# A diffusion layer on one core: the latent convolution in 32x32 tiles of the array, the layer norm by channels, and the scan's decay rows on ScalarE's queue

## The chip, the core and the metric

The kernel runs on one core of a Trainium2 chip. A core has five engines with instruction queues of their own: TensorE (PE; its weight loads are shown as PEld), VectorE (DVE), ScalarE (ACT), GpSimd (POOL) and SyncE (SP), which only issues transfers here. Transfers run on 16 DMA engines. The metric is the device time of one execution in microseconds (us), the median of several runs.

## The reference

One layer of a hybrid backbone, for 256 context tokens and 2048 latent tokens (a grid of 32 rows by 64 columns), model width 1024. Both go through the same weights:

```python
h = rms_norm(x, g_pre) * (1 + scale) + shift
u = h @ w_in
z, xbc, dt_raw, ga, gb, gsil = jnp.split(u, [...], axis=-1)
y_ssd, h_fin = ssd_branch(z, xbc, dt_raw, ...)          # scan in chunks of 128 tokens, both directions
# conformer_branch:
h = ga * jax.nn.sigmoid(gb)
h = depthwise_conv(h, conv_w, conv_b)                   # 31 taps along the grid's rows
h = layer_norm(h, ln_g, ln_b)                           # over the 1024 channels of a token
y_conf = jax.nn.silu(h) * jax.nn.silu(gsil)
out = jnp.concatenate([y_ssd, y_conf], axis=-1) @ w_out
return x + gate * rms_norm(out, g_post), h_fin
```

For latent tokens the convolution runs down the 32 rows of the grid, for each channel and each of 64 columns by itself. With 31 taps every one of the 32 rows reaches nearly every other, so one channel is a 32x32 matrix applied to a 32x64 block.

## The kernel before

Tokens are 18 tiles of 128 (two of context, 16 latent). The wide projections are made in three matmuls of 128x512 for each block of the contraction (high and low part of the operand: `mm_cm`, lines 378 to 380), the output projection likewise (`out_part`, line 1078: 96 matmuls a tile). The stages, by the trace:

- to about 340 us: modulation, normalised input, the scan's input channels for half 0 of the tokens (ten tiles);
- 340 to 720: `ga`, `gb` and the gates of half 0 (`gab_unit`, `silu_unit`); between their matmuls the scan of tiles 0 to 8 (`pass_a`) and half of the context convolution are interleaved;
- 720 to 945: the scan's channels for half 1;
- 945 to 1340: `ga`, `gb` and gates of half 1, interleaved with the scan of tiles 9 to 17, the latent convolution (`lat_conv`, eight channel blocks of 128) and the rest of the context convolution (`ctx_conv`);
- 1340 to 1430: the last gates, and `w_out` loaded and split;
- 1430 to the end: the final loop over 18 tiles: finish the scan's output (`ssd_pre`, `ssd_norm`, `ssd_scale`), normalise the convolution's (`conf_pre`, `conf_act`), project, add.

The names that matter below: `kd` is the kernel matrix data of a channel block as loaded, `kbuf` its expansion to block-diagonal 128x128 matrices of four channels (16 ScalarE copies of 32 partitions a block, line 622; the buffers are zeroed once by POOL), `cx` the block's input, `cp` the PSUM bank that a group of eight matmuls fills (line 634: the input is stationary, 128x64, the matrix moves), `cvv` the result with bias (line 639). The result has tokens on partitions and is stored as rows of tokens, `CVL`; for context `CVC`, after two transposes (line 595). In the final loop `conf_pre` loads a tile's tokens `cn`, takes mean and variance with VectorE's statistics instructions (1042, 1044), scales (1047), and `conf_act` transposes to channels with eight matmuls (1058) and applies SiLU with gain and bias from PSUM (1061).

In the scan, `load_lb` (line 664) broadcasts four decay rows to a tile `lb` of 128x512, 144 loads in all, eight a tile; POOL masks one direction (676), ScalarE takes exponentials (684, 673), VectorE multiplies (688), PE uses them as weights (720). `lb` has four buffers a direction.

All transfers are issued by SP, in order. The order of work on each engine is set by a scheduler that simulates the engines when the program is built; the interleaving of the source (`interleave`, `merge`) is what it starts from.

## Time and profile before

| | |
|---|---|
| median of 3 runs | 1882.09 us (1880.9 to 1887.08) |
| the profiled execution | 1882.2 us, span 1880.5 us |
| granted TensorE clock, mean | 0.986 |
| DMA, mean over the span | 200 GB/s, 375.29 MB |

"Busy" counts an engine's working instructions; waiting and the issue of transfers aren't counted. In a group row stand the source line, the engine, the operation, output and inputs, shapes, the count, then busy us and mean ns of one, then the idle time of the engine just before such instructions and what ended most of it. An fp32 matmul leaves two records, so the count of matmul records is twice that of instructions for those; the 128x512 matmuls of the projections and the transposes leave one. `SPq` is SP's own queue.

### The profile page before, as it was taken

Reading aid. Unit: us, or ns where it says so; the run is one execution under the profiler, and the core shown is the slowest. Engines: PE = TensorE matmul, PEld = TensorE weight load, DVE = VectorE, ACT = ScalarE, POOL = GpSimd, SP = SyncE. Lnnn points to the kernel's source line nnn. Section 1 sums busy time; section 2 is a strip of 40 time slices with the busy share of each in tenths; the row PEclk is TensorE's granted clock in tenths of the full one; section 3 lists DMA queues with packets and bytes.
Section 4 is the critical chain, followed back from the end, with each engine's and each line's share of the span. In section 5 each row is a group of like instructions: output and inputs, shape, how many; then the busy total and the mean of one; then the engine's idle time right before and its main releaser. Section 6 shows DMA issues by size and latency. Waiting matters only on the chain.

```text
span 1880.5 us, 26833 instructions
## 1 busy us (share of the span) xinstructions
PE 1825.6 (97%) x9739; PEld 1504.6 (80%) x9739; DVE 1188.2 (63%) x1699; ACT 839.5 (45%) x1786; POOL 269.0 (14%) x351
## 2 busy tenths in 40 slices
PE   7899999999999999999999899999999999999998
PEld 4788887787887888888877677777887888888887
DVE  2477887776545553577585768655427676766662
ACT  3646424443455441644355666675414232232321
POOL 0002001111111100100001011110013333333220
PEclk9899999999999999999999999999999999999999
DMA  8556575564677754545587897978887655555532
GB/s 302 212 200 198 211 239 179 176 222 155 211 269 225 225 200 169 165 154 188 179 195 215 210 242 194 278 185 234 239 268 239 191 174 173 165 172 173 175 102 78
DMA packets 290400, 375.29 MB, mean 200 GB/s; under 512 B 85206, under 2 KB 187478, under 8 KB 290268
## 3 DMA queue, kind: packets, MB, share of 16 engines
q1 hardware_dynamic: 290268, 373.58, 64.2%
q8 instruction: 77, 1.26, 0.3%
q14 instruction: 55, 0.45, 0.1%
HBM read 243.92 MB, written 129.59 MB: 199 GB/s over the span
## 4 chain that ended last, share of the span: by engine, by line
PE 62%; DMA 5%; ACT 3%; issue 3%; DVE 2%; SPq 2%; POOL 0%; POOLq 0%; DVEq 0%; ACTq 0%
PE op L1078 20%; PE sp L378 6%; PE sp L379 6%; PE sp L380 6%; DMA lb<-lt 3%; PE xp L379 2%; PE xp L378 2%; PE xp L380 2%; PE py L720 2%; PE ga L378 2%; PE ga L380 1%; PE po L727 1%; PE ga L379 1%; PE qo L985 1%; PE gb L378 1%
## 5 line engine op out<-in xcount | busy, mean ns | idle before, releaser
L684 ACT ACTIVATE lb<-lb,WB 128x128 f32<-128x128 f32 x576 | 184.1, 391 | 150.9 <-POOL lb L676 149.0
L378 PE MATMUL sp<-hh,wh 128*128 128x512 f32 (+1 forms) x640 | 239.7, 375 | 2.6 <-DVE sth L550 2.6
L379 PE MATMUL sp<-hl,wh 128*128 128x512 f32 (+1 forms) x640 | 237.0, 370 | 0.0
L380 PE MATMUL sp<-hh,wl 128*128 128x512 f32 (+1 forms) x640 | 236.7, 370 | 0.2 <-DMA wl<-wld 0.2
L676 POOL TENSOR_SCALAR_AFFINE_SELECT lb<-lb 128x512 f32<-128x512 f32 x144 | 108.7, 760 | 749.7 <-ACT el L673 416.1
L378 PE MATMUL xp<-hh,wh 128*128 128x512 f32 (+1 forms) x480 | 179.1, 375 | 6.1 <-ACT wh L353 4.0
L379 PE MATMUL xp<-hl,wh 128*128 128x512 f32 (+1 forms) x480 | 179.1, 373 | 0.2 <-DVE hl L299 0.2
L380 PE MATMUL xp<-hh,wl 128*128 128x512 f32 (+1 forms) x480 | 179.2, 374 | 0.0
L475 DVE SCALAR_TENSOR_TENSOR cva<-raw,cwh,cva 128x1280 f32<-128x1280 f32 (+1 forms) x96 | 142.7, 1495 | 15.5 <-ACT cva L469 13.6
L378 PEld LDWEIGHTS sp<-hh,wh 128*128 128x128 f32 x640 | 121.0, 189 | 24.3 <-DVE sth L550 3.1
L380 PEld LDWEIGHTS sp<-hh,wl 128*128 128x128 f32 x640 | 121.0, 189 | 21.6 <-DMA wl<-wld 0.7
L379 PEld LDWEIGHTS sp<-hl,wh 128*128 128x128 f32 x640 | 121.2, 189 | 20.1 <-issue 0.5
L378 PE MATMUL gb<-hh,wh 128*128 128x512 f32 (+1 forms) x320 | 121.9, 381 | 3.4 <-DVE gth L539 3.4
L378 PE MATMUL ga<-hh,wh 128*128 128x512 f32 (+1 forms) x320 | 120.4, 376 | 2.6 <-ACT gth L536 2.6
L379 PE MATMUL gb<-hl,wh 128*128 128x512 f32 (+1 forms) x320 | 119.3, 373 | 0.0
L380 PE MATMUL gb<-hh,wl 128*128 128x512 f32 (+1 forms) x320 | 119.1, 372 | 0.0
L380 PE MATMUL ga<-hh,wl 128*128 128x512 f32 (+1 forms) x320 | 118.1, 369 | 0.0
L379 PE MATMUL ga<-hl,wh 128*128 128x512 f32 (+1 forms) x320 | 117.9, 369 | 0.0
L590 DVE SCALAR_TENSOR_TENSOR cg<-cg,cv 128x256 f32<-128x256 f32 x240 | 113.3, 497 | 2.5
L550 DVE SCALAR_TENSOR_TENSOR sth<-sth,sp 128x512 f32<-128x512 f32 (+1 forms) x80 | 50.4, 630 | 98.4 <-ACT sth L549 98.4
L378 PEld LDWEIGHTS xp<-hh,wh 128*128 128x128 f32 x480 | 92.0, 192 | 23.0 <-ACT wh L353 4.8
L688 DVE TENSOR_TENSOR lb<-lb,lb 128x512 f32<-128x512 f32 x72 | 51.6, 717 | 85.6 <-ACT lb L684 55.8
(219 smaller groups left out, 3860.8 us busy)
## 6 DMA issues: line engine op xcount, KB each, us to landing
lb<-lt SPq DMA_DIRECT2D x144, 256.0 KB, 4.2
wr<-in_w_in SPq DMA_DIRECT2D x88, 256.0 KB, 4.9
whd<-wh SPq DMA_DIRECT2D x44, 512.0 KB, 3.4
wld<-wl SPq DMA_DIRECT2D x44, 512.0 KB, 4.7
wh<-whd SPq DMA_DIRECT2D x44, 512.0 KB, 5.2
wl<-wld SPq DMA_DIRECT2D x44, 512.0 KB, 5.6
xT<-xb SPq DMA_DIRECT2D x18, 512.0 KB, 5.4
yp<-yg SPq DMA_DIRECT2D x36, 256.0 KB, 4.5
```

The lines of the kernel that those rows point to most:

```text
L378: T.matmul(ps[:, :BN], wh[:, k, :], hh[:, k, :], start=(k == 0), stop=False)
L379: T.matmul(ps[:, :BN], wh[:, k, :], hl[:, k, :], start=False, stop=False)
L380: T.matmul(ps[:, :BN], wl[:, k, :], hh[:, k, :], start=False, stop=(k == KT - 1))
L475: V.scalar_tensor_tensor(a[:, :n], raw[:, t:t + n], cwh[:, ct * 5 + t:ct * 5 + t + 1], a[:, :n], MUL, ADD)
L550: V.scalar_tensor_tensor(th, th, 1.0, ps[:, :BN], ADD, MUL)
L590: V.scalar_tensor_tensor(acc, g[:, t:t + 256], cv[:, w0 + t:w0 + t + 1], acc, MUL, ADD)
L676: G.affine_select(E[g, hq, d], E[g, hq, d], pattern=[[0, 4], [sg, P]], compare_op=ALU.is_ge, fill=NEG, base=0, channel_multiplier=-sg)
L684: S.activation(lb[:, h, :], lb[:, h, :], AF.Exp, bias=WB[:, i, c + h:c + h + 1])
L688: V.tensor_tensor(a, a, E[g, hq, 1], ADD)
L720: T.matmul(py[g][j * HD:(j + 1) * HD, q * P:(q + 1) * P], xt[g][:, h * HD:(h + 1) * HD], E[g, hq, 0][:, t, :], start=True, stop=True)
L727: T.matmul(po[g][:, q * P:(q + 1) * P], Sf[g][:, q * P:(q + 1) * P], bc[:, 2 + g, :], start=True, stop=True)
L1078: T.matmul(pso[n], lhs[:, k % 8, :], w[:, n * 512:(n + 1) * 512], start=(k == 0 and m == 0), stop=(k == 15 and m == 2))
```

## The change

Three things are changed.

**The latent convolution.** Each matrix of 32x32 is now used as it is: stationary, on one 32x32 tile of the array, with the channel's input (32x64) moving. Partitions of `kd` and `cx` hold four groups `a` of channels with 32 rows of the grid each; the output's partitions are four groups `u`. A channel block is two half-groups of 64 matmuls: eight positions `q`, four `u` (columns of the array), two `a` (rows of the array, each into a PSUM bank of its own). One ScalarE copy a block turns the kernel around (`kt`); `cx` comes in 16 transfers, `kd` in 4, both for the next block ahead if its `GL` is complete; the bias is loaded once. The result has channels on partitions and goes to one tensor `CV` of channels by tokens, in 8 transfers a block. `ctx_conv` writes its rows there without transposes.

**The layer norm.** A tile is loaded with channels on partitions (`conf_load`), eight blocks of 128 tokens. `conf_mean` folds the eight blocks in three VectorE additions (`sum8`), adds over partitions and spreads the sum with one matmul against ones, and subtracts. `conf_var` squares (ScalarE), folds, and makes the variance a column of one value per token with a matmul of one column; POOL takes the power −1/2. `conf_scale` turns the column into a row on all partitions with a matmul against the identity, and multiplies. SiLU then reads SBUF. `ssd_pre`'s sum of squares uses `sum8` too, where it had one reduction (line 991).

**The decay rows.** `load_lb` issues from ScalarE's queue.

The body of `lat_conv` that goes stands in the listing above and is not repeated. Two spacers in memory and the places at which `out_part` is divided are changed with it.

```diff
     ZS = [dram(f"zs{h}", [D, HT[h] * P]) for h in range(2)]
     GL = [dram(f"gl{j}", [P, NT * P]) for j in range(KT)]
     GS = [dram(f"gs{h}", [D, HT[h] * P]) for h in range(2)]
-    CVC = dram("cvc", [NCTX * P, D])
-    CVL = dram("cvl", [LAT, D])
+    CV = dram("cv", [D, NT * P])
...
                 yield
-        ps = bank("ss", f"cps{j}")
-        for t in range(2):
-            T.transpose(ps[:, t * P:(t + 1) * P], acc[:, t * P:(t + 1) * P], ident)
         o = g[:, 768:1024]
-        S.mul(o, ps[:, :256], 0.5)
-        DMA.dma_start(CVC[:, j * P:(j + 1) * P].rearrange("(t p) c -> p t c", p=P),
-                      o.rearrange("p (t c) -> p t c", c=P))
-        yield
+        S.mul(o, acc, 0.5)
+        DMA.dma_start(CV[j * P:(j + 1) * P, 0:256], o)
...
+    def lat_load(j, lp):
+        kd = lp.tile([P, 32, 32], F32, tag="kd", name=f"kd{j}", bufs=2)
+        x = lp.tile([P, 32, 64], F32, tag="cx", name=f"cx{j}", bufs=2)
+        lat_in[j] = kd, x
+        for a in range(4):
+            rs = slice(a * 32, (a + 1) * 32)
+            src = bass.AP(tensor=wconv.tensor, offset=(j * 4 + a) * 64 * 32, ap=[[32, 32], [1, 1024]])
+            DMA.dma_start(kd[rs].rearrange("p r g -> p (r g)"), src)
+            for u in range(4):
+                c0 = u * 32 + a * 8
+                DMA.dma_start(x[rs, u * 8:(u + 1) * 8, :],
+                              GL[j][c0:c0 + 8, 256:].rearrange("c (r w) -> r c w", w=64))
+    def lat_conv(j, lp, cbb, more):
+        if j not in lat_in:
+            lat_load(j, lp)
+        kd, x = lat_in.pop(j)
+        yield
+        kt = lp.tile([P, 32, 32], F32, tag="kt", name=f"kt{j}", bufs=1)
+        S.copy(kt[:, :, ::-1].rearrange("p g r -> p r g"), kd)
+        if more(j + 1):
+            lat_load(j + 1, lp)
+        yield
+        vt = lp.tile([P, 32, 64], F32, tag="cvv", name=f"cvv{j}", bufs=1)
         for h in range(2):
+            ps = {a: bank("ss", f"cp{j}_{a}") for a in (2 * h, 2 * h + 1)}
+            for q in range(8):
+                for u in range(4):
+                    for a in ps:
+                        rs = slice(a * 32, (a + 1) * 32)
+                        T.matmul(ps[a][u * 32:(u + 1) * 32, q * 64:(q + 1) * 64], kt[rs, u * 8 + q, :], x[rs, u * 8 + q, :],
+                                 start=True, stop=True)
             yield
+            for a in ps:
+                V.scalar_tensor_tensor(vt[:, a * 8:(a + 1) * 8, :], ps[a].rearrange("p (c w) -> p c w", w=64), 0.5,
+                                       cbb[:, j, a * 8:(a + 1) * 8].unsqueeze(2).to_broadcast([P, 8, 64]), MUL, ADD)
+            for u in range(4):
+                c0 = j * P + u * 32 + h * 16
+                DMA.dma_start(CV[c0:c0 + 16, 256:].rearrange("c (r w) -> r c w", w=64),
+                              vt[u * 32:(u + 1) * 32, h * 16:(h + 1) * 16, :])
...
@@ -661,7 +663,7 @@
             for d in range(2):
                 lb = pa.tile([P, 4, P], F32, tag=f"lb{d}", name=f"lb{i}{g}{hq}{d}", bufs=4)
                 r0 = il * 32 + d * NH + g * 8 + hq * 4
-                DMA.dma_start(lb.rearrange("p h l -> p (h l)"),
+                S.dma_start(lb.rearrange("p h l -> p (h l)"),
                               LT[half][r0:r0 + 4, :].rearrange("h l -> (h l)").partition_broadcast(P))
...
-    kbuf = [lp.tile([P, 8, P], F32, name=f"kbuf{u}") for u in range(2)]
-    for u in range(2):
-        G.memset(kbuf[u], 0.0)
+    cbb = lp.tile([P, 8, 32], F32, name="cbb")
+    for u in range(4):
+        DMA.dma_start(cbb[u * 32:(u + 1) * 32],
+                      conf_b.rearrange("(j u n) -> u j n", u=4, n=32)[u].partition_broadcast(32))
     blocks = post(1, 5)
     cg = lambda name: lp.tile([P, D], F32, tag="cg", name=name, bufs=2)
-    extra = chain(f for j in range(4) for f in (lat_conv(2 * j, lp, kbuf), ctx_conv(j + 4, cg), lat_conv(2 * j + 1, lp, kbuf)))
+    lat = lambda j: lat_conv(j, lp, cbb, gl_done.__contains__)
+    extra = chain(f for j in range(4) for f in (lat(2 * j), ctx_conv(j + 4, cg), lat(2 * j + 1)))
...
+    def sum8(t, v):
+        V.tensor_tensor(t, v[:, 0:4, :], v[:, 4:8, :], ADD)
+        V.tensor_tensor(t[:, 0:2, :], t[:, 0:2, :], t[:, 2:4, :], ADD)
+        V.tensor_tensor(t[:, 0, :], t[:, 0, :], t[:, 1, :], ADD)
+        return t[:, 0, :]
...
-        zr = p1.tile([P, P], F32, tag="zr", name=f"zr{i}", bufs=2)
-        V.tensor_reduce(zr, z.rearrange("p q l -> p l q"), mybir.AxisListType.X, ADD)
+        zr = sum8(z[:, 0:4, :], z)
...
-    def conf_pre(i):
-        n = p2.tile([P, D], F32, tag="cn", name=f"cn{i}", bufs=1)
-        DMA.dma_start(n, CVC[i * P:(i + 1) * P, :] if i < 2 else CVL[(i - 2) * P:(i - 1) * P, :])
-        bs = p2.tile([P, 12], F32, tag="bs", name=f"bs{i}", bufs=2)
-        for h in range(2):
-            V.bn_stats(bs[:, 6 * h:6 * h + 6], n[:, h * 512:(h + 1) * 512])
-        mv = p2.tile([P, 2], F32, tag="mv", name=f"mv{i}", bufs=2)
-        V.bn_aggr(mv, bs)
-        V.tensor_scalar(mv[:, 1:2], mv[:, 1:2], EPS, None, ADD)
-        r = rstd_of(p2, mv[:, 1:2], f"cr{i}")
-        V.tensor_scalar(n, n, mv[:, 0:1], r, SUB, MUL)
+    rows8 = lambda t: t.unsqueeze(1).to_broadcast([P, 8, P])
+    def conf_load(i):
+        n = p2.tile([P, 8, P], F32, tag="cn", name=f"cn{i}", bufs=1)
+        DMA.dma_start(n, CV[:, i * P:(i + 1) * P].rearrange("(c p) t -> p c t", p=P))
         return n
 
-    def conf_act(i, n):
+    def conf_mean(i, n):
+        v = p2.tile([P, 8, P], F32, tag="v", name=f"v{i}", bufs=1)
+        t = sum8(v[:, 0:4, :], n)
+        mean = bank("ss", f"cm{i}")[:, 0:P]
+        T.matmul(mean, ones, t, start=True, stop=True)
+        V.scalar_tensor_tensor(n, rows8(mean), -1.0 / D, n, MUL, ADD)
+        return n, v
+    def conf_var(i, nv):
+        n, v = nv
+        S.activation(v, n, AF.Square)
+        t = sum8(v[:, 0:4, :], v)
+        pq = bank("ss", f"cq{i}")
+        T.matmul(pq[:, 0:1], t, ones[:, 0:1], start=True, stop=True)
+        ms = p2.tile([P, 1], F32, tag="cms", name=f"cms{i}", bufs=2)
+        V.tensor_scalar(ms, pq[:, 0:1], 1.0 / D, EPS, MUL, ADD)
+        return n, v, rstd_of(p2, ms, f"cr{i}"), pq
+    def conf_scale(i, nvr):
+        n, v, r, pq = nvr
+        T.matmul(pq[:, P:2 * P], r.to_broadcast([P, P]), ident, start=True, stop=True)
+        V.tensor_tensor(n, n, rows8(pq[:, P:2 * P]), MUL)
+        return n, v
+    def conf_act(i, nv):
+        n, v = nv
         gs = p2.tile([P, 8, P], F32, tag="gs", name=f"gsl{i}", bufs=1)
         DMA.dma_start(gs, chan_slice(GS, i))
-        v = p2.tile([P, 8, P], F32, tag="v", name=f"v{i}", bufs=1)
-        for g in range(2):
-            ps = bank("ss", f"ct{i}{g}")
-            for c in range(4):
-                k = 4 * g + c
-                T.transpose(ps[:, c * P:(c + 1) * P], n[:, k * P:(k + 1) * P], ident)
-            for c in range(4):
-                k = 4 * g + c
-                S.activation(v[:, k, :], ps[:, c * P:(c + 1) * P], AF.Silu, bias=cv[:, C_LNB + k:C_LNB + k + 1],
-                             scale=cv[:, C_LNG + k:C_LNG + k + 1])
+        for k in range(8):
+            S.activation(v[:, k, :], n[:, k, :], AF.Silu, bias=cv[:, C_LNB + k:C_LNB + k + 1],
+                         scale=cv[:, C_LNG + k:C_LNG + k + 1])
         V.scalar_tensor_tensor(v, v, 0.5, gs, MUL, MUL)
...
+                gap(p2, 64)
                 yh = ssd_scale(i, yr)
-                nrm = conf_pre(i)
+                nrm = conf_mean(i, conf_load(i))
...
-    v = conf_act(i, nrm)
+    v = conf_act(i, conf_scale(i, conf_var(i, nrm)))
...
-            n = conf_pre(nxt)
-        out_part(pso[i], yh, 3, 6)
+            n = conf_load(nxt)
+        out_part(pso[i], yh, 3, 5)
         if not last:
             yhn = ssd_scale(nxt, yr)
-        out_part(pso[i], yh, 6, 8)
+        out_part(pso[i], yh, 5, 7)
+        if not last:
+            n = conf_mean(nxt, n)
+        out_part(pso[i], yh, 7, 8)
         out_part(pso[i], pt, 8, 10)
         if last:
             out_part(pso[i], pt, 10, 16, (0,))
             out_part(pso[i], pt, 10, 16, (1,))
         else:
-            v = conf_act(nxt, n)
-            out_part(pso[i], pt, 10, 16)
+            n = conf_var(nxt, n)
+            out_part(pso[i], pt, 10, 12)
+            v = conf_act(nxt, conf_scale(nxt, n))
+            out_part(pso[i], pt, 12, 16)
...
-    wconv = wpad.reshape(8, 32, 4, 64).transpose(0, 2, 3, 1)
+    wconv = wpad.reshape(8, 4, 4, 8, 64).transpose(0, 2, 4, 1, 3)
```

In the second scan stage, on TensorE, the convolution stands between matmuls of the projection (`ga`, `hh`, `hl`, `wh`, `wl`; the changed kernel's lines 377 to 379 are 378 to 380 of before). Before:

```order
L380 MATMUL ga_1_4_8687<-hh_7343,wl_1_8345 128x512
L634 MATMUL cp_0_8691<-kbuf_8337,cx_8634 64x128 x8
L378 MATMUL ga_1_4_8687<-hh_7343,wh_1_8346 128x512
L379 MATMUL ga_1_4_8687<-hl_7344,wh_1_8346 128x512
L380 MATMUL ga_1_4_8687<-hh_7343,wl_1_8345 128x512
```

After:

```order
L379 MATMUL ga_1_4_8681<-hh_7330,wl_1_8333 128x512
L637 MATMUL cp_0_8686<-cx_8615,kt_8642 32x64
L637 MATMUL cp_1_8687<-cx_8615,kt_8642 32x64
L637 MATMUL cp_0_8686<-cx_8615,kt_8642 32x64
L637 MATMUL cp_1_8687<-cx_8615,kt_8642 32x64
```

The two banks alternate to 64 matmuls in one run, and then the projection goes on; there are 16 such runs where there were 32 of eight.

On ScalarE, in the first scan stage (`xwh` is a cast of the scan's input, `el` the exponential kept for later, `gth` a gate's eviction). Before:

```order
L710 CAST xwh_4602<-xw_4601 128x512
L673 ACTIVATE el_4680<-lb_4761 64x256 x2
L684 ACTIVATE lb_4761<-lb_4761,WB 128x128 x4
L710 CAST xwh_4669<-xw_4668 128x512
L749 COPY sb_4755<-pst_4660 128x512
```

After:

```order
L712 CAST xwh_4102<-xw_4101 128x512
L675 ACTIVATE el_4180<-lb_4244 64x256 x2
L686 ACTIVATE lb_4244<-lb_4244,WB 128x128 x4
L538 ACTIVATE gth_6_1_4135<-gb_6_1_4077 128x512
L666 DMA lb_4756<-lt_115 128x512
L686 ACTIVATE lb_4756<-lb_4756,WB 128x128 x4
L666 DMA lb_4296<-lt_115 128x512
L712 CAST xwh_4169<-xw_4168 128x512
```

The loads of `lb`, which stood on SP, stand between ScalarE's exponentials, casts and evictions.

On TensorE in the final loop (`op` the output's two banks, `yh`, `yl`, `ph`, `pl` the operands' parts, `pm` the scan norm's sums, `ct` the transposed tile, `cq` the variance and its spread). Before, the eight transposes:

```order
L1078 MATMUL op_0_14882<-woh_13066,pl_14879 128x512
L1078 MATMUL op_1_14883<-woh_13066,pl_14879 128x512
L1058 MATMUL ct_15002<-ident,cn_14940 128x128 x4
L1058 MATMUL ct_15011<-ident,cn_14940 128x128 x4
L1078 MATMUL op_0_14882<-woh_13072,ph_14878 128x512
```

After, around the spread of the scale:

```order
L1100 MATMUL op_1_15636<-wol_13435,yh_15517 128x512
L1074 MATMUL cq_15562<-ident,cr_15566 128x128
L1100 MATMUL op_0_15635<-woh_13436,yl_15518 128x512
L1100 MATMUL op_1_15636<-woh_13436,yl_15518 128x512
L1100 MATMUL op_0_15635<-woh_13475,yh_15517 128x512
```

The transposes are gone; the matmul of the variance stands ahead of the scan's `pm` and `qo`, that of the scale eight matmuls behind them, and before a tile's `ph` part the first matmuls of the next tile (`op_0` alone) are placed.

More of the change, by code (lines that the diff above doesn't have):

```diff
@@ L526, in xbc_phase @@
             pass
+    gl_done = set()
     def gab_unit(half, j, hb):
@@ L530, in gab_unit @@
         wa = next_w()
+        gl_done.discard(j)
         for b in ORDER[half]:
@@ L540, in gab_unit @@
             DMA.dma_start(GL[j][:, o:o + BN], th)
+        if half:
+            gl_done.add(j)
     def silu_unit(half, c0, dst, j, hb, order=None):
@@ new lines, in backbone_kernel @@
+    lat_in = {}
+    def lat_load(j, lp):
[10 more added lines that the diff above has]
+                              GL[j][c0:c0 + 8, 256:].rearrange("c (r w) -> r c w", w=64))
@@ new lines, in lat_conv @@
+    def lat_conv(j, lp, cbb, more):
[9 more added lines that the diff above has]
+        vt = lp.tile([P, 32, 64], F32, tag="cvv", name=f"cvv{j}", bufs=1)
+        for h in range(2):
+            ps = {a: bank("ss", f"cp{j}_{a}") for a in (2 * h, 2 * h + 1)}
[5 more added lines that the diff above has]
+                                 start=True, stop=True)
+            yield
+            for a in ps:
[5 more added lines that the diff above has]
+                              vt[u * 32:(u + 1) * 32, h * 16:(h + 1) * 16, :])
+            yield
@@ L1035, in load_gg @@
         gg[a] = t
-    def conf_pre(i):
-        n = p2.tile([P, D], F32, tag="cn", name=f"cn{i}", bufs=1)
-        DMA.dma_start(n, CVC[i * P:(i + 1) * P, :] if i < 2 else CVL[(i - 2) * P:(i - 1) * P, :])
-        bs = p2.tile([P, 12], F32, tag="bs", name=f"bs{i}", bufs=2)
-        for h in range(2):
-            V.bn_stats(bs[:, 6 * h:6 * h + 6], n[:, h * 512:(h + 1) * 512])
-        mv = p2.tile([P, 2], F32, tag="mv", name=f"mv{i}", bufs=2)
-        V.bn_aggr(mv, bs)
-        V.tensor_scalar(mv[:, 1:2], mv[:, 1:2], EPS, None, ADD)
-        r = rstd_of(p2, mv[:, 1:2], f"cr{i}")
-        V.tensor_scalar(n, n, mv[:, 0:1], r, SUB, MUL)
-        return n
@@ L1126, in backbone_kernel @@
                 p2 = ph_1.enter_context(tc.tile_pool(name="p2", bufs=1))
-                gap(p2, 192)
+                gap(p2, 64)
                 yh = ssd_scale(i, yr)
-                nrm = conf_pre(i)
+                nrm = conf_mean(i, conf_load(i))
     for u in last:
         run(u)
-    v = conf_act(i, nrm)
+    v = conf_act(i, conf_scale(i, conf_var(i, nrm)))
     ph_b[2].close()
```

36 lines of the change are left out of this document (removed).

## The prediction

> **What bounds the kernel now.** I read the busy shares first, then the chain of waits, then the windows by stage. The columns of the first row are busy us, share of the span, instructions.
>
> ```profile
> PE 1825.6 (97%) x9739; PEld 1504.6 (80%) x9739; DVE 1188.2 (63%) x1699; ACT 839.5 (45%) x1786; POOL 269.0 (14%) x351
> PE 62%; DMA 5%; ACT 3%; issue 3%; DVE 2%; SPq 2%; POOL 0%; POOLq 0%; DVEq 0%; ACTq 0%
> ```
>
> TensorE is busy 97% of the 1880.5 us span; no other engine passes 63%. The chain agrees: most of it is PE, and all else on it is small. So a change can win by taking work off PE, or by closing PE's pauses, and loses by opening new ones. The windows say where pauses are (first and last us, length, busy us of each engine with instructions, granted clock, DMA share, GB/s):
>
> ```profile
> 440.00:560.00 120.00, 117.72 (x676) 98.50 (x675) 62.54 (x110) 59.00 (x147) 15.82 (x21) 1.00 0.68 223
> 560.00:700.00 140.00, 137.37 (x776) 115.16 (x776) 76.11 (x126) 70.03 (x176) 13.43 (x19) 0.99 0.66 215
> 945.00:1060.00 115.00, 109.87 (x634) 85.79 (x633) 91.60 (x172) 65.03 (x147) 11.78 (x18) 0.97 0.78 196
> 1060.00:1200.00 140.00, 131.59 (x813) 103.97 (x812) 92.89 (x150) 91.01 (x213) 17.47 (x27) 0.98 0.86 226
> 1200.00:1340.00 140.00, 136.09 (x818) 106.09 (x817) 81.26 (x118) 88.06 (x191) 13.29 (x19) 0.99 0.79 226
> 1500.00:1600.00 100.00, 100.00 (x498) 84.35 (x497) 68.99 (x81) 28.96 (x60) 33.87 (x28) 1.00 0.58 178
> PE cp L634 <- ACT kbuf L622: 10.0, 6, 2.7
> PE cp L634 <- DMA cx<-gl: 1.9, 1, 1.9
> ```
>
> In the second scan stage (945 to 1340) PE idles 395 − 377.55 = 17.5 us, and the two wait rows (us, times, longest) give 11.9 of it to the latent convolution, which waits for its expanded kernel or its input. In the first scan stage (440 to 700) PE idles 4.9 us. In the final loop (1500 to 1600) it has no pause at all: there only fewer or shorter matmuls help.
>
> **The convolution on PE.** A group before is 8 matmuls, each with two records, in two column halves of the array:
>
> ```profile
> 957.30 0.39 PE L379 MATMUL ga<-hl,wh 128*128 128x512 f32 x1
> 957.53 0.39 PE L380 MATMUL ga<-hh,wl 128*128 128x512 f32 x1
> 957.85 1.09 PE L634 MATMUL cp<-kbuf,cx 128*64 128x128 f32 x16
> 958.87 0.50 PE L378 MATMUL ga<-hh,wh 128*128 128x512 f32 x1
> 959.21 0.40 PE L379 MATMUL ga<-hl,wh 128*128 128x512 f32 x1
> 957.85 0.33 PE L634 MATMUL cp<-kbuf,cx 128*64 128x128 f32 x2
> 33.27 0.61 PE L239 MATMUL mp<-wm,sc 128*2 128x256 f32 x8 [0.75 <-DMA wm<-in_w_mod]
> L634 PE MATMUL cp<-kbuf,cx 128*64 128x128 f32 x512 | 37.1, 291 | 12.4 <-ACT kbuf L622 10.0 <-DMA cx<-gl 1.9 <-DVE cvv L639 0.3
> ```
>
> In the plain stream matmuls start 0.227 us apart. From 957.53 to 959.21 are 1.68 us for two such steps and the group, so a group costs 1.68 − 0.45 = 1.23 us, some 0.35 of it change of shape on entry and exit, 0.88 streaming: eight records one behind the other in each half, 110 ns each for 128 columns. The halves do run side by side: two records of 291 ns each are over in 0.33. 32 groups: 39.5 us.
>
> After, a group is 64 matmuls of 32x32 with 64 columns: eight tiles of the array (two row groups by four column groups), each with 8 × 2 = 16 records. Half the columns is about 55 ns, so 16 × 55 = 0.88 us if the eight tiles run side by side, and with 0.35 again 1.23 us, but for 16 groups only: 19.7 us, **−19.8**. That four column tiles overlap is seen at 33.27, where eight records of some 460 ns end within 0.61. That two row groups do, no row shows. If they take turns a group is 2 × 0.88 + 0.35 = 2.11, 33.8 in all, −5.7. If every record took the 64 ns that a record has on average today (1.02 us by 16), 2048 records are 131 us and the edit costs +97. I take side by side, since columns behave so and the two row groups write different banks.
>
> A rule of the Trainium skill speaks against it: "TensorE: Matmul & The Clock Gate", "Wait — 56ns, not 53.3ns?", says that matmuls never start less than about 25 ns apart, however few their columns. Taken over all tiles this gives 2048 × 25 ns = 51 us, 57 with the switches, +17 instead of −19.8. The halves' records here (two within 0.33 us) are too few to decide; the same page's "Packing small matmuls — row/col tiling" puts different tiles about 4 ns apart, by which −19.8 stands.
>
> **The waits in front of it.** The 16 expanding copies per channel block become one, and inputs are fetched a block ahead. 11.9 us of PE's waits lose their cause; what can be late next is that one copy, or the column of loads ahead of it. I take **−10** (bounds 0, where another engine is late in its place, and −17.5, where every pause of this stage closes).
>
> **Context convolution.** Two transposes per block go. Eight of the kind hold PE 0.79 us in the rows below and delay what follows by 0.09, so a pair is 0.20 to 0.29; I take 0.23, 8 × 0.23 = **−1.8**.
>
> **The final loop on PE.** Eight transposes per tile go; three small matmuls come (mean, variance, spread of the scale).
>
> ```profile
> 1519.84 0.62 PE L1078 MATMUL op<-woh,pl 128*128 128x512 f32 x2
> 1520.30 1.03 PE L1058 MATMUL ct<-ident,cn 128*128 128x128 f32 x8
> 1521.09 0.70 PE L1078 MATMUL op<-woh,ph 128*128 128x512 f32 x2
> 1505.74 0.28 PE L1004 MATMUL pm<-ones,zr 128*128 128x1 f32 x2
> 1505.88 0.71 PE L1078 MATMUL op<-woh,yh 128*128 128x512 f32 x2
> L1004 PE MATMUL pm<-ones,zr x16: 164/207/250, 1505.7 to 1680.7; 128*128 128x1 f32 x16
> ```
>
> The transposes hold PE 0.79 us and delay the next pair 0.09 (0.70 against 0.62): 0.88. One small matmul holds it 0.14 and the same 0.09: 0.23, three 0.68. Net −0.2 per tile; the period is (1680.7 − 1505.7) / 7 = 25.0 us, so 24.8 after. Over 17 tiles **−3.5**, provided PE stays the limit. That hangs on VectorE, which now has the whole layer norm:
>
> ```profile
> L991 DVE TENSOR_REDUCE zr<-z 128x128 f32<-128x1024 f32 x18 | 36.2, 2011 | 1.1 <-ACT z L989 1.1
> L1042 DVE BATCH_NORM_STATS2 bs<-cn 128x6 f32<-128x512 f32 x36 | 23.2, 685 | 19.9 <-DMA cn<-cvl 19.3 <-DMA cn<-cvc 0.6
> L1047 DVE TENSOR_SCALAR cn<-cn,mv,cr 128x1024 f32<-128x1024 f32 x18 | 14.6, 813 | 11.1 <-POOL cr L135 11.1
> L1013 DVE TENSOR_TENSOR y<-y,pm 128x1024 f32<-128x1024 f32 x18 | 21.8, 1209 | 2.9 <-PE pm L1012 2.9
> L986 DVE TENSOR_TENSOR elb<-elb,qo 128x512 f32<-128x512 f32 x34 | 21.9, 681 | 7.1 <-DMA elb<-el 5.7 <-PE qo L985 1.4
> L989 ACT ACTIVATE z<-y 128x1024 f32<-128x1024 f32 x18 | 19.1, 1062 | 144.9 <-DVE y L988 144.8
> ```
>
> Removed per tile: 2.01 + 2 × 0.69 + 0.81 + about 0.36 of short ones = 4.56. Added: three folds of 512, 256 and 128 columns, by the 0.68 of `L986` and fractions of it about 1.4 each, two passes over 1024 at 1.21 (`L1013`), one short: 6.8. From 69.0 busy us in four periods, 17.2 per tile, VectorE goes to 19.5. In-order waits come on top: for the mean's matmul, for the square (1.06 on ScalarE) and for the variance's matmul, some 3 us where nothing is put between. 22.5 of 24.8: it fits, with little left. The longer chain also stands once uncovered, in front of the first tile, and some tiles will slip: **+3** (bounds 0 and +34, below).
>
> **Decay rows on ScalarE's queue.**
>
> ```profile
> L622 ACT COPY kbuf<-kd 32x256 f32<-32x256 f32 x128 | 83.3, 657 | 19.6 <-DMA kd<-in_wconv 11.8 <-PE cp L634 6.0
> L664 SPq DMA_DIRECT2D lb<-lt x144: 319/360/2937, 152.2 to 1291.4; - x144
> SPq L664 <- DVE lb L688: 117.5, 43, 8.6
> SPq L664 <- PE py L720: 17.9, 15, 2.2
> SPq L664 <- DVE hl L299: 10.5, 8, 3.8
> ACT lb L684 <- POOL lb L676: 149.0, 72, 7.8
> ```
> The issue row gives the shortest, median and longest ns, and first and last start. 144 issues of at least 0.36 us are 52 us that move to ScalarE (more where one takes up to 2.9). With them go the waits for a free buffer: 117.5 + 17.9 + 10.5 = 146 us in which SP stood until VectorE or TensorE had done with the rows. ScalarE is in order: behind such a wait stand the evictions of the projections, the casts of the scan and the exponentials of the next rows. Its own work falls at the same time: 83.3 us of copies go, eight copies of 1024 columns come (by `L622` between 1.05 and 2.6 us each, I take 2: 16). So busy time is about even (−67 + 52), and what remains is the 146 us of standing. In the two scan stages ScalarE is busy 129 of 260 and 244 of 395 us, so 282 us are idle, and part of the standing falls into them: `lb L684` waits 149 us for POOL there, which is the same pipeline a step later. On the other side SP loses 146 us of standing in front of the other loads, and the rows can come sooner. I take **+6**: PE's 4.9 us of pauses in the first scan stage doubled, and a little in the second; bounds −15 (all that is left of PE's 22.4 us of pauses in both stages after the step above, −10, shared) and +40 (below).
>
> **Sum** against the profiled execution's 1882.2 us (span 1880.5; it lies at the median 1882.09): −19.8 − 10 − 1.8 − 3.5 + 3 + 6 = −26.1, so **1856 us**. Inside this case 1842 to 1872.
>
> **The rivals.**
> - *Row groups take turns.* The convolution saves 5.7, not 19.8: 1870. For it: no row shows two row groups at once. Against: the column halves start together. 0.11.
> - *Tiles are issued one by one.* Records below the streaming time cost their issue. The row's 64 ns each gives 1856 + 19.8 + 97 = 1973, zero extra gives 1856; for a case in which half the overlap is lost, 1915. 0.05. By the 25 ns of the page cited above it would be 1856 + 19.8 + 17 = 1893.
> - *ScalarE stands for its rows* (the slower side). Place: the two scan stages, from the point at which the wait for a free `lb` outlasts ScalarE's slack. Of 146 us a share like its busy share (129/260 = 0.50, 244/395 = 0.62) falls on time it needs, 73 to 90 us of evictions and casts pushed back; a wait is at most 8.6 us long, and a projection unit is 24 × 0.227 = 5.4 us of PE's work that can go on before a bank is missing, so I let half through: 40 instead of 6, 1890. For it: ScalarE is the engine on the chain after DMA, and PE has no slack. Against: much of the standing falls when the work on the rows waits anyway (the 149 us). 0.15.
> - *The final loop becomes VectorE's.* If two more waits of some 1 us and the slower pace beside POOL bring the 22.5 to 26.5 us, the period grows by 1.7 over 24.8: 17 × 1.7 = 29, less the 3 taken, 1882; at 27 us, 1890. I give 1886. For it: 17.2 + 2.3 and three engines in a row. Against: 24.8 is wider than the sum. 0.08.
> - *The scan stage's gain is swallowed.* DMA's share there is 0.78 to 0.86; the work is the same in bytes, so a shorter stage raises it to 0.9. If the loads then set the pace, both large terms shrink to a third (−10 in all): 1876. 0.12.
> - *The rows come sooner.* SP freed of the waits closes PE's pauses in both stages (the other bound, −15 in place of +6, partly): 1842. 0.06.
>
> **How the numbers follow.** The forecast has 0.43. This kernel's runs can tell 0.3% (5.6 us) from no change, so faster is below 1876.4, slower above 1887.7. Faster: 0.43 + 0.11 + 0.06, half of the swallowed gain 0.06 and a small part of the rest 0.03: 0.69. Slower: tiles one by one 0.04, ScalarE 0.10, the final loop 0.04, and 0.02 of the others: 0.20. Same: 0.11. The range from 1838 to 1890 holds the forecast, the turns, the swallowed gain and the lower part of the two slower cases; outside stay the one-by-one case, the worse half of ScalarE's and a few hundredths below.
>
> **What would show it.** Right: convolution groups of 128 records that hold PE about 1.2 us, PE's waits on the convolution gone from the second scan stage, a period of 24.8 us in the final loop with PE at 100%, ScalarE's new waits for `lb` not named before PE's pauses. Wrong: a group of 2 us or more; PE waiting in the scan stages for tiles that ScalarE evicts or casts, with the `lb` issue as what ScalarE did before; PE pausing in the final loop for the mean, the variance or `ph`; pauses at the same places as now with DMA as releaser.

## The result, and the profile after

The changed kernel takes 2008.5 us (median of 4 runs, 2005.9 to 2012.9) against 1882.4 for the kernel before: a ratio of 1.067, 95% interval 1.064 to 1.070. The forecast was 1856, the range 1838 to 1890. The profiled execution has a span of 2005.6 us, 125 more than before.

Busy shares and chain of the changed kernel:

```profile
PE 1858.8 (93%) x11223; PEld 1518.1 (76%) x11223; DVE 1201.2 (60%) x1807; ACT 798.1 (40%) x1684; POOL 254.3 (13%) x349
PE 65%; DMA 13%; DVE 9%; issue 6%; ACT 5%; POOL 3%; SPq 0%; POOLq 0%; ACTq 0%; DVEq 0%
```

No engine took PE's place as the busiest: DVE even has a smaller share than before. What grew is PE's idle time, and the shares of DMA and DVE on the chain. Two windows, and from the list of waits the three largest of PE in the final loop (us, times, longest), tell where:

```profile
940.00:1345.00 405.00, 371.02 (x3782) 292.80 (x3781) 256.64 (x442) 178.27 (x437) 43.41 (x64) 0.96 0.76 214
1500.00:1800.00 300.00, 258.61 (x1170) 208.93 (x1168) 175.57 (x249) 82.39 (x158) 75.35 (x70) 0.92 0.52 139
```

```profile
PE op L1100 <- ACT yh L1029: 53.5, 16, 6.3
PE op L1100 <- ACT ph L1091: 13.1, 8, 3.3
PE op L1100 <- DVE yl L1030: 5.3, 8, 2.3
```

In the final loop (second row) PE is busy 258.6 of 300 us, at a granted clock of 0.92; before it was busy all the time, at 1.00. The waits are for `yh` and `ph`, the operands of the output projection itself. In the second scan stage (first row) PE idles 34 us where it idled 17.5 (387.55 busy of the same 405).

The period of the final loop, from the scan norm's matmul (two records a tile), before and after in this order:

```profile
L1004 PE MATMUL pm<-ones,zr x30: 164/207/250, 1480.7 to 1828.9; 128*128 128x1 f32 x30
```

```profile
L1014 PE MATMUL pm<-ones,z x32: 164/250/250, 1475.2 to 1946.0; 128*128 128x1 f32 x32
```

348.2 us for 14 periods are 24.9 a tile before, 470.8 for 15 are 31.4 now: 6.5 × 17 or 18 steps, 111 to 117 us, is nearly the whole loss. Up to the last gate (1419.0 before, 1425.1 now) the kernel lost 6 us, where 25.6 less were forecast (−19.8 − 10 − 1.8 + 6).

The convolution itself, in the same place as shown of before:

```profile
952.16 0.39 PE L379 MATMUL ga<-hh,wl 128*128 128x512 f32 x1
952.48 1.47 PE L637 MATMUL cp<-cx,kt 32*32 32x64 f32 x128
953.88 0.50 PE L377 MATMUL ga<-hh,wh 128*128 128x512 f32 x1
954.22 0.40 PE L378 MATMUL ga<-hl,wh 128*128 128x512 f32 x1
```

A group of 128 records costs 954.22 − 952.16 − 0.45 = 1.61 us, 16 of them 25.7. The tiles do run side by side, if not as closely as assumed: in the trace 29 of the 128 records start in the first 0.22 us of this group (952.48 to 952.70). If the two row groups took turns, four records every 55 ns, it would be at most 20. Later in the group two records start every 17 ns, so that it takes 1.40 us and not 0.88; what holds these back was not followed.

### The profile page after: what moved, and what is told of

It reads as the page before. It is cut to its first block, busy times and chain, and to the rows that moved or that the text cites. A ratio compares the mean times of both kernels' runs of the same rounds, so it can differ in the third digit from the quotient of the medians.

```text
span 2005.6 us, 29934 instructions
## 1 busy us (share of the span) xinstructions
PE 1858.8 (93%) x11223; PEld 1518.1 (76%) x11223; DVE 1201.2 (60%) x1807; ACT 798.1 (40%) x1684; POOL 254.3 (13%) x349
## 4 chain that ended last, share of the span: by engine, by line
PE 65%; DMA 13%; DVE 9%; issue 6%; ACT 5%; POOL 3%; SPq 0%; POOLq 0%; ACTq 0%; DVEq 0%
PE op L1100 16%; DMA lb<-lt 6%; PE sp L377 6%; PE sp L379 6%; PE sp L378 6%; PE xp L377 4%; PE xp L378 4%; PE xp L379 4%; PE gb L377 2%; PE ga L377 2%; PE gb L378 2%; PE gb L379 2%; PE ga L378 2%; PE ga L379 2%; ACT lb L686 1%
## 5 line engine op out<-in xcount | busy, mean ns | idle before, releaser
L1100 PE MATMUL op<-woh,yh 128*128 128x512 f32 x288 | 115.3, 448 | 56.8 <-ACT yh L1029 56.8
L378 PEld LDWEIGHTS sp<-hl,wh 128*128 128x128 f32 x640 | 121.0, 189 | 19.8
L1100 PE MATMUL op<-woh,yl 128*128 128x512 f32 x288 | 112.3, 435 | 5.3 <-DVE yl L1030 5.3
L1100 PEld LDWEIGHTS op<-woh,yh 128*128 128x128 f32 x288 | 60.5, 213 | 74.6 <-ACT yh L1029 63.7
```

Source lines behind the costliest of these rows:

```text
L378: T.matmul(ps[:, :BN], wh[:, k, :], hl[:, k, :], start=False, stop=False)
L1100: T.matmul(pso[n], lhs[:, k % 8, :], w[:, n * 512:(n + 1) * 512], start=(k == 0 and m == 0), stop=(k == 15 and m == 2))
```

## The experiments

**One part at a time.** Theory after the result: the final loop's loss is the layer norm's, the scan stage's that of the queue, which eats what the convolution saves. Rivals: the convolution brings losses of its own; the queue is free; the loop is slow for its loads. Three runs make one change each, one undoes one.

The convolution alone:

```diff
 # the changed kernel, with before's conf_pre / conf_act, reading the same bytes as token rows
-                S.dma_start(lb.rearrange(
+                DMA.dma_start(lb.rearrange(
```

> Only the convolution in 32x32 tiles (with the context convolution's rows); the layer norm is that of before and reads the channel rows as if they were token rows (same bytes, the values are not the layer norm's), the decay rows are loaded by SP. Theory (the final loop's loss is the layer norm's, the convolution saves 32 x 1.23 - 16 x 1.60 = 13.8 us of PE and closes about 10 us of pauses): 1855 to 1870. Rival (the tiles bring losses of their own in the scan stage, by their loads and waits): 1880 or more.

Measured: 1884.7, ratio 1.003 (1.002 to 1.004). The rival is right: the convolution alone gains nothing.

```diff
 # the kernel before
-                DMA.dma_start(lb.rearrange(
+                S.dma_start(lb.rearrange(
```

> The kernel before with the decay rows' 144 loads on ScalarE's queue and nothing else. Theory (ScalarE stands in its queue for free buffers, and PE's evictions behind it): slower by 15 to 40 us, 1897 to 1922, with new PE pauses between 340 and 1340. Rival (the move is free, the scan stage's loss has another cause): 1877 to 1888.

Measured: 1878.3, ratio 1.000 (0.998 to 1.001). The move is free, and the theory fails in this part: SP's 146 us of standing do not become standing of ScalarE that PE feels.

```diff
 # the kernel before, with conf_load, conf_mean, conf_var, conf_scale and sum8 of the change
```

> The kernel before with the layer norm by channels (and the sum of squares by folds) alone; it reads the token rows' bytes as if they were channel rows, so its values are not the layer norm's. Theory (the final loop's period is set by the in-order waits between PE and VectorE that the norm brings): period near 32 us in place of 25, 1990 to 2010. Rival (the loop is slow for its loads of 512-byte rows, or for what the convolution left behind): with this loop alone the period stays below 27 us, 1880 to 1920.

Measured: 2001.8, ratio 1.065 (1.063 to 1.067); the period is 31.3. The layer norm alone makes the loop slow, without the convolution and the queue.

```diff
 # the changed kernel
-                S.dma_start(lb.rearrange(
+                DMA.dma_start(lb.rearrange(
```

> The changed kernel with the decay rows' loads back on SP. Theory: the final loop stays at 32 us a tile, the scan stages end about 25 us earlier than in the changed kernel: 1975 to 1990. Rival (the queue is free): within 6 us of the changed kernel, 2002 to 2014.

Measured: 2002.7, ratio 1.065 (1.062 to 1.067): 6 us below the changed kernel, with overlapping intervals. The rival holds here too.

**Why the convolution gains nothing alone.** Its trace shows ScalarE waiting for decay rows in the second scan stage, and SP issuing the inputs in a row. ScalarE's wait in that stage before, then with the convolution alone, then SP's queue there (start, us, instructions):

```profile
ACT el L673 <- DMA lb<-lt: 28.2, 12, 6.1
```

```profile
ACT el L676 <- DMA lb<-lt: 103.4, 18, 11.2
```

```profile
1099.63 4.29 SPq L618 DMA_DIRECT2D cx<-gl  x9
1104.02 0.39 SPq L667 DMA_DIRECT2D lb<-lt  x1
1104.45 3.39 SPq L618 DMA_DIRECT2D cx<-gl  x7
```

Each issue here holds SP about 0.48 us; 16 input loads hold it 7.7 us, and a load of decay rows stands among them. The next kernel deals the channels to the tiles in another way (channel 4g + a to row group a), so that the same bytes in the same 256-byte runs need 12 transfers a block and not 28.

```diff
-            for u in range(4):
-                DMA.dma_start(x[rs, u * 8:(u + 1) * 8, :], GL[j][c0:c0 + 8, 256:]...)
+            DMA.dma_start(x[rs], GL[j][:, 256:].rearrange("(g c) (r w) -> c r g w", c=4, w=64)[a])
+            # outputs: one store per u for both halves; kernel and bias in the same order
```

> As the run with the convolution alone, but the channels dealt to the tiles so that a block has 12 transfers (4 kernel, 4 input, 4 output) in place of 28, with the same bytes and the same 256-byte runs; the layer norm again reads the wrong rows. Theory (SP needs about 0.48 us for each issue, and the decay rows stand behind 16 input loads in a row): the conv's saving shows, 1860 to 1872. Rival (the second scan stage is paced by the scan's own chain of steps, and PE's saved time becomes waiting): no change against that run, 1879 to 1889.

Measured: 1870.2, ratio 0.994 (0.992 to 0.996); ScalarE's wait for the rows falls from 103.4 to 56.3 us:

```profile
ACT el L675 <- DMA lb<-lt: 56.3, 18, 6.2
```

The number of issues was the cause of most of it: 14.5 us between the two medians (17 by the ratios, each taken beside the kernel before) for 128 issues; the bytes are the same, and so is the time of an eviction, 0.68 us. The kernel before also had 12 transfers a block and a wait of 28.2, so a part of ScalarE's wait has another cause.

```diff
     def lat_conv(j, lp, cbb, more):
+        return
```

> The kernel before with the latent convolution left out whole (no loads, matmuls, evictions or stores; the layer norm reads other rows of the same size). If PE's work sets the second scan stage: 39.5 us of PE and 11.9 us of waits less than before, 1825 to 1838. If the scan's chain of steps sets it: the stage keeps most of its length with more PE pauses, 1850 or more.

Measured: 1817.7, ratio 0.966 (0.964 to 0.968), even below the first range. The windows of that run:

```profile
940.00:1060.00 120.00, 120.00 (x635) 96.59 (x634) 63.51 (x97) 56.48 (x150) 14.30 (x21) 1.00 0.63 198
1060.00:1200.00 140.00, 140.00 (x748) 111.96 (x748) 83.75 (x129) 77.57 (x211) 23.42 (x32) 1.00 0.65 212
1200.00:1345.00 145.00, 145.00 (x713) 118.38 (x712) 69.29 (x95) 46.66 (x91) 12.40 (x13) 1.00 0.65 219
```

Without the convolution PE has no pause in the stage, and its clock is full. So the scan's own chain does not pace the stage. The old convolution cost 63 us, not the 39.5 of its matmuls (this run also makes the context convolution without transposes, forecast at 1.8); the new one with 12 transfers still costs 52, twice its matmuls' 25.7.

**The other way round.** The input stationary, the 32x32 matrix moving, so that tokens stay on partitions and the old layer norm serves.

```diff
-   T.matmul(ps[a][u * 32:..., q * 64:...], kt[rs, u * 8 + q, :], x[rs, u * 8 + q, :])
+   T.matmul(ps[a][h * 64:..., g * 32:...], x[rs, h * 16 + g, :], kt[rs, h * 16 + g, :])
```

> The kernel before with the latent convolution in 32-row tiles, but the input stationary (32x64) and the 32x32 matrix moving, so that the result keeps tokens on partitions and the layer norm stays as it was; 12 to 13 transfers a block, nothing left out. By the theory of SP's issues: 1860 to 1874. By the rival (the scan's chain sets the stage): 1876 to 1888.

Measured: 1946.5, ratio 1.034 (1.031 to 1.038), against both expectations.

```profile
PE cp L643 <- DVE cvv L647: 20.9, 8, 9.5
PE px L704 <- issue: 10.7, 2, 8.7
```

A group now takes 2.0 us from its start to the next matmul, with half the columns of 1.4. It runs on four tiles (two row groups, two column halves) where the other form has eight, and four records start every 58 ns (28 in the 0.41 us from 953.09 to 953.50), so that 32 such rounds are 1.9 us: a record of 32 columns takes no less than one of 64 does there. PE also waits for the evictions, which write single elements with a stride (1048 ns each, 682 in the changed kernel). But those of the kernel before took 1064 ns, so their length alone does not explain the 65 us; why these waits grow so long was not followed further.

**The final loop.** Theory: the scheduler places the variance's matmul behind nearly the whole `ph` block and the next tile's `op_0` matmuls ahead of that block; variance and scan norm then come due at one point, VectorE stands before it and has everything to do after it. PE's rows in the changed kernel at one such point (`cq<-ones` the variance, `pm<-ones` the scan norm's sum, `pm<-ident` the spread of its result, which `yh` of the next tile needs):

```profile
1629.52 0.61 PE L1100 MATMUL op<-wol,ph 128*128 128x512 f32 x2
1629.97 0.28 PE L1067 MATMUL cq<-ones,v 128*128 128x1 f32 x2
1630.11 0.70 PE L1100 MATMUL op<-woh,pl 128*128 128x512 f32 x2
...
1631.35 0.28 PE L1014 MATMUL pm<-ones,z 128*128 128x1 f32 x2
...
1636.36 0.38 PE L1022 MATMUL pm<-ident,yr 128*128 128x128 f32 x2
...
1640.41 0.74 PE L1100 MATMUL op<-woh,yh 128*128 128x512 f32 x2 [0.91 <-ACT yh L1029]
1640.99 0.63 PE L1100 MATMUL op<-wol,yh 128*128 128x512 f32 x2
1643.16 0.73 PE L1100 MATMUL op<-woh,ph 128*128 128x512 f32 x2 [1.53 <-ACT ph L1091]
```

VectorE's rows there, and its waits over the loop:

```profile
1630.29 0.16 DVE L1069 TENSOR_SCALAR cms<-cq 128x1 f32<-128x1 f32 x1 [4.88 <-PE cq L1067]
1631.66 0.16 DVE L1016 TENSOR_SCALAR yms<-pm 128x1 f32<-128x1 f32 x1 [1.22 <-PE pm L1014]
...
1633.00 1.41 DVE L1116 SCALAR_TENSOR_TENSOR o<-op,or,gg 128x512 f32<-128x512 f32 x2 [0.68 <-POOL or L134]
```

```profile
DVE cn L1059 <- PE cm L1058: 59.4, 15, 6.5
DVE cms L1069 <- PE cq L1067: 56.0, 12, 4.9
```

VectorE waits 59.4 + 56.0 us in the loop for two small matmuls which have their operands (the fold ends 4.9 us before) and stand in PE's queue; then PE waits for `yh`, which stands in VectorE's. The first attempt makes load, mean and variance a tile earlier, with more buffers.

```diff
+            n2 = conf_scale(nxt, nv)                 # early in the tile
+            m = conf_load(order[a + 2]) ... conf_mean(order[a + 2], m) ... conf_var(order[a + 2], m)
```

> The run with the layer norm alone, but load, mean and variance are made one tile earlier, with two buffers of the loaded tile and a buffer of their own for the squares; the same instructions per tile. Theory (variance and scan norm come due at one point, so that both chains start behind one block of matmuls): period 25 to 27 us, 1880 to 1925. Rival (VectorE's added work or the lower clock sets the period): period above 30 us, 1980 or more.

Measured: 1973.2, ratio 1.048 (1.045 to 1.051), a period of 29.2: between the expectations. Only every other tile stops now, and its row shows the second price of a pause:

```profile
1666.30 0.62 PE L1100 MATMUL op<-woh,pl 128*128 128x512 f32 x2
1671.49 0.80 PE L1100 MATMUL op<-woh,yh 128*128 128x512 f32 x1 [4.58 <-ACT yh L1027]
1672.09 0.63 PE L1100 MATMUL op<-wol,yh 128*128 128x512 f32 x1
1672.76 0.80 PE L1100 MATMUL op<-woh,yl 128*128 128x512 f32 x1
```

After 4.6 us of waiting the matmuls start 0.4 to 0.7 us apart for some 5 us, where 0.23 is usual; the granted clock from 1674 to 1676 is 0.50. Next, the changed kernel with PE's order in the loop held to the source's, by an edge (a dependency added when the program is built) that asks for order only:

```diff
-                    T.matmul(pso[n], ...)
+                    K(T.matmul(pso[n], ...))      # K = tc.keep_in_program_order; all matmuls from ssd_pre to out_part
```

> The changed kernel, instruction for instruction, with TensorE's order in the final loop held to that of the source (scan norm after 6 and 30 of a tile's 96 matmuls, mean after 42, variance after 60, scale after 72); nothing else is held. Theory (the loop is slow because the built order puts variance and scan norm behind one block and the next tile's matmuls ahead, so that PE stands and its clock falls after each pause): period near 25 us, 1885 to 1900. Rival (VectorE's added work or the waits of the chain as such set the period): period above 28 us, 1935 or more.

Measured: 1963.3, ratio 1.043 (1.039 to 1.046), period 28.5. The same instructions in another order on one engine give 45 us back, not the 115 expected: the rival's range, so PE's order alone was not the cause. Two more runs join the parts, with PE's order still held:

> TensorE's order held as above, the convolution with 12 transfers a block, the decay rows on SP: the whole layer in its new form, nothing left out. If the parts add (before 1881, the convolution with 12 transfers -11, the layer norm's three matmuls for eight transposes -3.5 where PE sets the loop): 1862 to 1874. If the layer norm keeps a cost of its own with the order held: 1880 or more.

> The same with the decay rows on ScalarE's queue. If the queue matters little (alone it moved nothing): within 6 us of the run beside it. If SP's column of loads still delays the rows: 5 to 10 us faster. If ScalarE stands for its buffers: 5 us or more slower.

Measured: 1943.3 (ratio 1.033, 1.031 to 1.035) and 1937.8 (1.030, 1.028 to 1.032): the layer norm kept a cost of its own. The queue gained 5.5 us, which lies in two of its three expectations and decides nothing. In the first of the two runs, in the loop:

```profile
DVE cn L1075 <- PE cq L1074: 60.1, 17, 4.5
DVE v L1085 <- ACT v L1083: 55.5, 17, 3.3
```

VectorE now waits 3.5 us a tile for the scale and 3.3 for the SiLUs, with other work behind these steps in its queue. The period of this run, by the scan norm's matmul, is 28.6 us (400.0 us for 14 periods), not the 27.5 of the next expectation. Two runs move one of these waits each:

```diff
             out_part(pso[i], pt, 8, 10)
-            n = conf_var(nxt, n)
-            out_part(pso[i], pt, 10, 12)
+            out_part(pso[i], pt, 10, 11)
+            n = conf_var(nxt, n)
+            out_part(pso[i], pt, 11, 12)
```

> As the run with all three and TensorE's order held, with two changes: the order is held in the loop only (not for the first tile, where PE stood 10.7 us for the scan norm), and the variance's matmul stands after 66 and the scale's after 72 of the tile's matmuls (60 and 72 before), so that VectorE waits for the scale 1.4 us less. If VectorE's in-order waits set the period of 27.5 us: 26 us a tile, 1895 to 1920. If its busy time sets it: no shorter, 1925 or more.

Measured: 1910.0, ratio 1.016 (1.014 to 1.017), 26.5 a tile. As the waits would have it: 2.1 us less over 17 steps is 35 us, about the whole gain of 33.

```diff
     def conf_hl(i, vg):
+        K(V.scalar_tensor_tensor(v, v, 0.5, gs, MUL, MUL))     # was the end of conf_act
```

> As the run beside it, and the product with the gate (VectorE, which waited 3.3 us a tile for the eight SiLUs) is held behind the previous tile's last steps, where its input is long there; the same instructions. If VectorE's in-order waits set the period: 25 us a tile, TensorE without pauses in the loop, 1865 to 1890. If VectorE's busy time sets it: within 8 us of the run beside it.

Measured: 1997.6, ratio 1.062 (1.059 to 1.065), 32.0 a tile: the expectation failed.

```profile
PE cm L1059 <- DVE v L977: 69.7, 14, 5.8
```

PE waited for the next tile's fold, for which the buffer was now free too late. With two buffers, held and not held:

> As the run with the gate's product held later (which took 32 us a tile), with two buffers for the loaded tile and for its folds, so that the next tile's fold need not wait until VectorE has made the low part of this tile; the same instructions. If that run was slow because the fold came due behind a wait: TensorE's 5 us of waiting for the mean go, 25 to 27 us a tile, 1875 to 1905. If the held place itself is the cost (VectorE then waits for the previous tile's last matmuls before it can go on): 30 us a tile or more, 1965 or more.

> As the run with the variance's matmul close to the scale's (26.5 us a tile, 1910), with the same two pairs of buffers. If VectorE's wait for the SiLUs (3.2 us a tile) sets the rest, buffers change nothing there: 1903 to 1915. If the fold's lateness (1.2 us a tile at the variance's matmul) sets it: 25.5 us a tile or less, 1880 to 1895.

Measured: 1956.5 (1.039, 1.034 to 1.045) at 30.0 a tile, and 1915.7 (1.018, 1.017 to 1.020) at 27.2. PE's wait for the mean went in the first, as expected, but a wait of 46.6 us at the variance's matmul came, since VectorE stood 6.5 us a tile before the previous tile's last sums; buffers did not help the second, which came out at the upper edge of its first expectation. Each move took one wait away and made another step late, as long as the scheduler still placed VectorE's and ScalarE's instructions. So all three were held, in an order where each step that needs another engine's result has ready work ahead of it:

```diff
+        c = conf_fold(nxt, n)                         # start of the tile
+        step(fin); yr = ssd_norm(nxt, yz); pt, low = conf_hl(i, v, gs); step(fin); low(); step(fin)
+        ... c = conf_var(nxt, c)                      # after 54 matmuls
+        step(g)                                       # the scan's sum, between variance and scale
+        ... v = conf_act(nxt, c); yz = step(g)        # scale after 66; y * z behind the SiLUs
```

> The whole layer in its new form (convolution with 12 transfers, layer norm by channels, decay rows on SP), with the order held in the final loop on TensorE, VectorE and ScalarE: every step of VectorE that needs a matmul's or a SiLU's result stands behind other work that is ready (the gate's product at the start of the next tile, the scan's sums between variance and scale, the product with z behind the SiLUs), two buffers for the loaded tile and its folds; the same instructions per tile. If the in-order waits were the whole loss of the final loop: 24.8 to 25.3 us a tile with TensorE without pauses, 1865 to 1885. If the layer norm by channels has a cost that no order takes away (VectorE's busy time, slower beside POOL): 26 us a tile or more, 1895 or more.

Measured: 1879.1, ratio 0.999 (0.997 to 1.001), in the first expectation. The loop by its window, by the scan norm's matmul, and PE's longest wait from the last gates on:

```profile
1500.00:1800.00 300.00, 300.00 (x1466) 252.36 (x1465) 225.91 (x314) 105.26 (x198) 106.82 (x80) 1.00 0.59 173
```

```profile
L1034 PE MATMUL pm<-ones,z x30: 164/207/250, 1480.1 to 1826.2; 128*128 128x1 f32 x30
```

```profile
PE pm L1034 <- DVE z L980: 12.7, 1, 12.7
```

PE is busy throughout, at full clock; 346.1 / 14 = 24.7 a tile. VectorE is busy 18.6 us a tile (225.91 / 300 × 24.7), as in the changed kernel (175.57 / 300 × 31.4 = 18.4): its work was never too much. The 12.7 us at the first tile remain. The last two runs free that tile's order:

```diff
-    K = lambda ins: tc.keep_in_program_order(ins) if hold else ins
+    K = lambda ins: tc.keep_in_program_order(ins) if hold and hold[-1] else ins
```

> As the run with the three engines' order held, but not for the first of the 18 tiles, where TensorE stood 12.7 us for the scan norm's sum (which ran at lower clock afterwards): the held order's only pause in the loop. If the parts add then (the convolution with 12 transfers -11, the loop's period that of before): 1862 to 1870. If the second scan stage or the first tile takes it back in another place: 1876 or more.

> The same with the decay rows on ScalarE's queue. By the pair of runs with all three parts (1943 and 1938): 3 to 8 us faster than the run beside it. By the run with the queue alone: within 3 us.

Measured: 1879.5, ratio 0.998 (0.997 to 0.999), against the expectation that the parts add, and, with the rows on ScalarE's queue, 1875.8, ratio 0.995 (0.994 to 0.997), 3.7 us less, as the earlier pair had it. This is the fastest kernel here with nothing left out, half a per cent below the kernel before. The 12.7 us did not come back as time: five shorter pauses stand at the first tile in their place (4.1, 3.3, 1.6, 1.3 and 0.8 us). From 1345 to 1500 PE idles 11.1 us in the first of these two runs and 3.5 in the run with the convolution in 12 transfers alone (1870.2), which is most of the 9 us between them: the layer norm by channels is not free at the loop's start.

## Why the prediction was wrong

**"It fits, with little left", the term of the final loop (−3.5, and +3 for what slips), is the step that failed.** It counted VectorE's busy time (19.5 us a tile forecast, 18.4 measured) and 3 us of waits, and compared the sum with PE's 24.8. The waits were not 3 us: in the changed kernel VectorE stands 59.4 + 56.0 us, some 7 us a tile, for the mean's and variance's matmuls alone, because these stand in PE's queue behind matmuls that have no hurry, and PE stands 71.9 us for what VectorE, and ScalarE behind it, makes late. The order was there to be read before the run: with the next tile's `op_0` matmuls ahead of the `ph` block, 16 to 27 matmuls of the projection stand between the scan norm's sum and the use of its result (24 in the rows above), where 90 stood between before. At the four tiles where PE stops for 6.3 us, only one stands between the spread of that result and its use. The text on the order ahead of the prediction says that the `op_0` matmuls come first, and the prediction's sum does not use it. That the loss is order and not work is shown by the run with three orders held, 24.7 us a tile with the same steps; more buffers alone had not shortened the loop.

**The rival had the place and not the size.** "The final loop becomes VectorE's" put 26.5 to 27 us a tile and 1886 at 0.08. It was 31.4. Missing were both queues waiting for each other, and the clock: 41.4 of 300 us are pauses (4.3 us a tile), and the granted clock of 0.92 makes the other 27 us about 2.2 longer; together 24.8 + 6.5.

**The convolution, −19.8.** The mechanism was right (two row groups side by side, shown by the starts in the trace), the size was off: 16 × 1.61 = 25.7 us, −13.8. The rules weighed beside it: the 25 ns that the Trainium skill's "TensorE: Matmul & The Clock Gate" gives ("Wait — 56ns, not 53.3ns?") as the least distance of two starts does not hold over different tiles, 1.40 us / 128 = 11 ns a record here, 22 a matmul; the 4 ns of its "Packing small matmuls — row/col tiling" are not reached either.

**Its waits, −10.** Wrong by sign. The 11.9 us at the old convolution's matmuls went, but with the convolution alone PE idles 33.5 us in the second scan stage (371.5 busy of 405) where it idled 17.5, most of it at the scan's own matmuls. "The column of loads ahead of it" was named as what could be late next, with a bound of 0; it was the column of issues on SP that delayed others' loads, a loss (1884.7 alone, against 1870.2 with fewer issues, where PE idles 20.4 us in that stage: still more than before). The prediction counted the conv's transfers in bytes and did not multiply the extra issues by SP's time for one.

**Decay rows, +6.** The run alone shows 0, within 0.2%; in the changed kernel the move cost at most 6 us, and with 12 transfers it gained 5.5 and 3.7. The rows of SP's waiting were no measure of what ScalarE would wait; the mechanism of that rival did not appear. The bound of −15 for this term was more than the 12.4 us of pauses that the step above it had left, and the 0.36 us of an issue, called the least, is the median.

**Context convolution, −1.8,** cannot be told apart in these runs. **The layer norm's −0.2 a tile on PE** is right once PE sets the pace: 24.87 before, 24.72 with the order held.

One reading did not touch the sum: the eight records at 33.27 take 379 ns each, not some 460.

What would show it wrong was listed: "PE pausing in the final loop for the mean, the variance or `ph`". It paused for `ph`, and mostly for `yh`, which was not named.

## What to carry to other kernels

An engine at 75% of the period is not safe if its steps and the bounding engine's alternate: draw where each small matmul stands in the queue, and what must be done between its result and its use. When steps are made finer, look at the built order of all engines before counting their time; holding one engine alone only moved the wait. Count transfers, not only bytes, on a queue that others use: 128 more issues at half a microsecond cost more than the matmuls saved.

## What the runs showed of the hardware

- 64 fp32 matmuls of a 32x32 matrix with 64 columns, on eight tiles, take 1.40 us (11 ns a record); with a 32x64 input stationary and 32 columns moving, on four tiles, 2.0 us: half the columns, more time.
- A pause of PE of 4.6 us is followed by some 5 us in which matmuls start about twice as far apart. In a loop this price (the clock of 0.92) came to a third of the loss. "HAM oscillation — how this bites in real kernels" on the page "TensorE: Matmul & The Clock Gate" of the Trainium skill tells of pauses over 3.4 us; in the changed kernel the loop's pauses are 4.3 us a tile together, in pieces of which the longest is 6.3. Shorter ones do it too: after the pauses of 0.9 and 1.5 us at 1640 and 1643 the granted clock from 1646 to 1648 is 0.50.
- The old convolution cost 63 us of the kernel's time with 39.5 us of matmuls: without it, TensorE had neither pauses nor low clock in that stage. How much of the 52 us of the form with 12 transfers comes from the load on the DMA engines (busy 0.78 to 0.88 of the time, against 0.63 to 0.65 without a convolution), and how much from VectorE's evictions, is open.
